# Feed-forward part of a hybrid decoder layer: order of two products, and which engine reads PSUM when

## The chip, the cores and the metric

One core of a Trainium2 chip runs the whole layer in one launch. The metric is device time in microseconds from the start of the launch to its end; the kernel before takes 745.95 us, the median of three runs (745.78 to 746.09).

## The reference, cut to what matters

The layer is a token mixer (attention and an mLSTM merged by gates) followed by a SwiGLU feed-forward part; the change is in the second. With 512 tokens, a model width of 1024 and a hidden width of 2816, all in float32:

```
h = h + merged @ w_out                       # token mixer, 512 x 1024
u = rms_norm(h, norm_ffn_g)
g, up = split(u @ w_gate_up)                 # 1024 -> 2 x 2816
h = h + (silu(g) * up) @ w_down              # 2816 -> 1024
out = rms_norm(h, norm_final_g)
```

## The kernel before

**Three products for one.** Every float32 operand is split into a high half (rounded to the format that TensorE multiplies at once) and a low half (the rest), so each product is three matmuls: high x high, low x high, high x low. ScalarE writes the high half of a weight tile (its copy in the helper `act_`, line 148 or 153), VectorE subtracts to get the low half (line 732 in the gated steps, 776 in the down steps).

**Seven products for eight.** The feed-forward matrices are multiplied as 2 x 2 blocks by a scheme of the Strassen-Winograd kind: seven block products named W11, S1, S2, W12, S3, S4, W22 after their weight operand, where S1 to S4 are sums of weight blocks made on VectorE (lines 740, 741 and 771). The sums of the results are formed partly by letting several products accumulate in one PSUM bank and reading partial sums out in between.

**Gated steps ("gu", 22 of them, one for each 128 hidden columns).** The blocks are halves of the 1024 inputs by halves of the tokens, and the two output blocks of a weight tile are gate and up. A product is 12 matmuls of 256 columns (`prod`, lines 784 to 786). X, one PSUM tile (pool `mm`, three buffers), first takes W11 and is copied to `s12` by ScalarE; then S2 is added into it and the sum copied again; then S3, copied to `x3` and added to Z on VectorE (line 835); then W22. Z (pool `s`, three buffers) takes S1 and later S4. Y (pool `acc`) takes W12. A product may only go on into a bank whose earlier sum has been read out. `gu_first` emits W11, `gu_main` S1 to S3, `gu_last` S4, W22 and the SiLU product, which goes through three or five more VectorE operations (even and odd steps) to the operands of the down product.

**Down steps ("ds", five).** Each takes four hidden tiles; a product is 2 token tiles x 6 matmuls of 512 columns (`ds_prod`, lines 897 to 899), with two X, two Z and the same chain of partial sums. Results are scaled by the tokens' inverse root mean square (`r`, `nr`) and added to the residual in DRAM by accumulating DMAs of GpSimd's queue. The last down step (`ds_end`) adds into the residual held in SBUF, takes in the last two hidden tiles by plain products (`last`), and ends with the final norm of four token blocks: VectorE's `add_`, ScalarE's `square`, Ln and Exp for the root, three VectorE operations (`newton`), then `apply` (one half on VectorE, one on ScalarE) and the DMA out.

**The order of work.** `plan` lays the products in a row and gives each a due time in ns: 1440 for a gated product, 2720 for a down product (two times 1360). `at(key, product, offset)` makes that time plus an offset the priority of the instructions that follow. A scheduler at build time fills each engine's queue by these priorities among what is ready by its own times; on the chip each queue runs in the order so fixed. Weights are prepared at offsets before their product (high half -1800, low half -800, sums -3800). Buffers are tiles from pools: ten tiles for split weights, seven for raw ones, 34 small ones.

The order of the products in a gated step, and the step between neighbours, is set in `plan`:

```
seq += [(x, w) for w in ("S1", "S2", "W12", "S3")]
after = [(ITEMS[j + 1], "W11")]
seq += (after if x[0] == "gu" else []) + [(x, w) for w in ("S4", "W22")] + (after if x[0] == "ds" else [])
```

Of the kernel before, what the change touches and what calls it, by code (L numbers as in the profile page):

```python
# [11 lines left out]
AF = mybir.ActivationFunctionType  # L12
# [59 lines left out]
NG = 5  # L72
DS_AFTER = {4: 0, 8: 1, 12: 2, 16: 3, 21: 4}

H_OFF, L_OFF, S_OFF, U_OFF, E_OFF, O_OFF, D_OFF, S4_OFF = 1800, 800, 3800, 0, 3000, 1500, 1500, 10000

PRE = 120

ITEMS = []
# [5 lines left out]
def hybrid_layer_kernel(ctx: ExitStack, tc, xT, wall, wgu, wds, wdl, g3v, vecs, wgates, consts, rope, out):  # L85
# [17 lines left out]
    def slot(dt=F32, name="a"):  # L103
        return act.tile([P, S], dt, name=nm(name), tag="A")
# [11 lines left out]
    def mmb():  # L116
        return psum.tile([P, S], F32, name=nm("mm"), tag="mm", bufs=3)

    def sb():
        return psum.tile([P, S], F32, name=nm("s"), tag="S", bufs=3)  # L120
# [25 lines left out]
    def act_(out_, in_, func, **kw):  # L146
        if func not in SETS:
            return A.activation(out_, in_, func, **kw)  # L148
        table(SETS[func])
        if ph["manual"]:  # L150
            return A.activation(out_, in_, func, **kw)
        with tc.issue_after(ph["load"]):
            i = A.activation(out_, in_, func, **kw)
        ph["ins"].append(raw_ins(i))
        return i
# [546 lines left out]
    def plan():  # L702

        t = 0
        LONG = {"W12": 4, "LAST": 1, "W22": 4, "S4": 5}
        seq = [(ITEMS[0], "W11")]
        for j, x in enumerate(ITEMS):
            if j == len(ITEMS) - 1:
                seq += [(x, w) for w in ("S1", "S2", "W12", "S3", "LAST", "W22", "S4")]
                continue  # L710
            seq += [(x, w) for w in ("S1", "S2", "W12", "S3")]
            after = [(ITEMS[j + 1], "W11")]
            seq += (after if x[0] == "gu" else []) + [(x, w) for w in ("S4", "W22")] + (after if x[0] == "ds" else [])
        for x, w in seq:
            clock["at"][x, w] = t
            t += 1440 if x[0] == "gu" else 1360 * LONG.get(w, 2) if x == ITEMS[-1] else 2720
        clock["end"] = t

    def at(key, w, off=0):
        t = clock["at"][key, w] + off  # L720
        tc.cur_priority = clock["base"] + (t if t > 0 else t // PRE)
# [56 lines left out]
    def prod(ps, w, o, first=False):  # L778

        wh, wl = w  # L780
        for k in range(4):
            c = slice(k * P, (k + 1) * P)
            bh, bl = bop(o, k)
            T.matmul(ps, wh[:, c], bh, start=first and k == 0, stop=False, skip_group_check=not first)  # L784
            T.matmul(ps, wl[:, c], bh, start=False, stop=False, skip_group_check=not first)  # L785
            T.matmul(ps, wh[:, c], bl, start=False, stop=k == 3, skip_group_check=not first)  # L786
# [3 lines left out]
    def gu_first(i):  # L790
        key = ("gu", i)
        g = sw[key]
        at(key, "W11")
        g["X"] = mmb()[:, 0:HS]
        prod(g["X"], g["W11"], 0, first=True)
        at(key, "S2")
        g["s"] = slot(name="s12")
        act_(g["s"][:, A_], g["X"], AF.Copy)

    def gu_main(i):  # L800

        key = ("gu", i)
        g = sw[key]
        x, s12 = g["X"], g["s"]
        at(key, "S1")
        z = g["Z"] = sb()[:, 0:HS]
        prod(z, g["S1"], 1, first=True)
        at(key, "S2")
        prod(x, g["S2"], 4)
        at(key, "S3")  # L810
        act_(s12[:, B_], x, AF.Copy)
        at(key, "W12")
        y = accb()[:, 0:HS]
        prod(y, g["W12"], 2, first=True)
        if i == 0:
            residual()
            rb2 = st["rb2"] = rstd_rows([ssum[2]])

            pr = sb()
            for t in range(4):  # L820
                T.transpose(pr[:, 4 * t : 4 * t + 4], rb2[0:4, t * P : (t + 1) * P], con[0:4, C_ID : C_ID + 4])
            st["rc"], st["nrc"] = (cst.tile([P, 4], F32, name=n_) for n_ in ("rc2", "nrc2"))
            V.tensor_copy(st["rc"], pr[:, 0:16:4])
            V.tensor_scalar(st["nrc"], pr[:, 0:16:4], -1.0, None, op0=ALU.mult)
        at(key, "W22", U_OFF)
        u = g["u"] = slot(name="up")
        V.tensor_tensor(u[:, A_], y, s12[:, A_], op=ALU.subtract)
        at(key, "S3")
        prod(x, g["S3"], 5)
        at(key, "S4")  # L830
        t = g["t"] = slot(name="gt")
        xs_ = slot(name="x3")[:, A_]
        act_(xs_, x, AF.Copy)
        at(key, "S4")
        V.tensor_tensor(t[:, B_], z, xs_, op=ALU.add)

# [69 lines left out]
    def ds_run(n):  # L908

        key = ("ds", n)  # L910
        w = sw.pop(key)["w"]
        r, nr = ([st[x][:, t : t + 1] for t in range(4)] for x in ("rc", "nrc"))
        Lo, Hi = slice(0, S), slice(S, D)
        to = lambda t, c, s: nc.gpsimd.dma_start(h1d[t][:, c], s, accum_op=ALU.add)
        two = range(2)
        X = [mmb() for t in two]
        s1, s2, x3 = [], [], []
        for t in two:
            at(key, "W11", 1360 * t)
            ds_prod(X[t], w["W11"], n, 0, t, first=True)  # L920
            at(key, "S2", 1360 * t)
            s1.append(slot(name="s1"))
            act_(s1[t], X[t], AF.Copy, scale=r[t])
        Z = [sb() for t in two]
        for t in two:
            at(key, "S1", 1360 * t)
            ds_prod(Z[t], w["S1"], n, 1, t, first=True)
        for t in two:
            at(key, "S2", 1360 * t)
            ds_prod(X[t], w["S2"], n, 4, t)  # L930
            at(key, "S3", 1360 * t)
            s2.append(slot(name="s2"))
            act_(s2[t], X[t], AF.Copy, scale=r[t + 2])
        for t in two:
            at(key, "W12", 1360 * t)
            y = accb()
            ds_prod(y, w["W12"], n, 2, t, first=True)
            at(key, "W12", 1360 * t + D_OFF)
            V.scalar_tensor_tensor(s1[t], y, r[t], s1[t], op0=ALU.mult, op1=ALU.subtract)
            to(t, Lo, s1[t])  # L940
        for t in two:
            at(key, "S3", 1360 * t)
            ds_prod(X[t], w["S3"], n, 5, t)
            at(key, "W22", 1360 * t)
            x3.append(slot(name="x3"))
            act_(x3[t], X[t], AF.Copy, scale=r[t + 2])
            at(key, "S4", 1360 * t)
            V.scalar_tensor_tensor(x3[t], Z[t], r[t + 2], x3[t], op0=ALU.mult, op1=ALU.add)
            to(t + 2, Hi, x3[t])
        for t in two:  # L950
            at(key, "S4", 1360 * t)
            ds_prod(Z[t], w["S4"], n, 3, t)
            at(key, "S4", 1360 * t + D_OFF)
            V.scalar_tensor_tensor(s2[t], Z[t], nr[t + 2], s2[t], op0=ALU.mult, op1=ALU.subtract)
            to(t + 2, Lo, s2[t])
        for t in two:
            at(key, "W22", 1360 * t)
            ds_prod(X[t], w["W22"], n, 6, t)
            at(key, "W22", 1360 * t + D_OFF)
            o = slot(name="c21")  # L960
            act_(o, X[t], AF.Copy, scale=r[t])
            to(t, Hi, o)
        hb[n] = None

    def ds_end():
# [12 lines left out]
        def add_(t, j, ps, c, d=slice(0, S)):  # L978

            h = hs[t][j][:, d]  # L980
            V.scalar_tensor_tensor(h, ps[:, d], c, h, op0=ALU.mult, op1=ALU.add)

        def square(t, j, d=slice(0, S)):
            s = v_()
# [24 lines left out]
        def last(ps, t, j, first=False, d=slice(0, S)):  # L1009

            q, c = slice(t * P, (t + 1) * P), slice(j * S + d.start, j * S + d.stop)
            for k in range(LK):
# [3 lines left out]
                T.matmul(ps[:, d], ah[:, q], wl[:, c], start=False, stop=False, **g)  # L1016
                T.matmul(ps[:, d], al[:, q], wh[:, c], start=False, stop=k == LK - 1, **g)

        X, Z = [mmb() for t in two], [sb() for t in two]
        for t in two:  # L1020
            at(key, "W11", U * t)
# [33 lines left out]
        for t in two:  # L1055
            at(key, "W22", 2 * U * t)
            ds_prod(X[t], w["W22"], n, 6, t)
            last(X[t], t, 1)
            at(key, "W22", 2 * U * t + 1000)
            times_g(t, 0)  # L1060
            at(key, "W22", 2 * U * (t + 1) + 200)
            add_(t, 1, X[t], r[t])
            square(t, 1)
            q, v, _ = rstd(t, "W22", 2 * U * (t + 1) + 2000)
            apply(t, newton(q, v, v_), 1)
        at(key, "S4")
        ds_prod(Z[0], w["S4"], n, 3, 0)
        last(Z[0], 2, 0)
# [2 lines left out]
        at(key, "S4", 2 * U + 200)  # L1071
        add_(2, 0, Z[0], nr[2])
        square(2, 0)
        q, v, _ = rstd(2, "S4", 2 * U + 2000)
        q2 = newton(q, v, v_)
        y = accb()
        lo, hi = slice(0, HS), slice(HS, S)
        at(key, "S4", 2 * U)
# [10 lines left out]
        at(key, "S4", 9 * U // 2)  # L1089
        last(y, 3, 1, first=True, d=hi)  # L1090
        at(key, "S4", 5 * U + 200)
        add_(3, 1, y, nr[3], hi)
        square(3, 1, hi)
        q, v, i = rstd(3, "S4", 5 * U + 800)
        with tc.issue_after(raw_ins(i[0])), tc.issue_after(raw_ins(i[1])):
            apply(2, q2, 0)
            times_g(3, 0)
        apply(3, newton(q, v, v_), 1)

# [527 lines left out]
```

## Time and profile before

| | |
|---|---|
| median of 3 runs | 745.95 us (745.78 to 746.09) |
| profiled execution | 745.64 us, of which the span from first to last instruction is 743.9 us |
| busy share of the span | TensorE matmul 99%, weight loads 86%, VectorE 84%, ScalarE 58%, GpSimd 8% |
| first feed-forward product, end of the last matmul | 400.3 us, 736.4 us |
| chain that ended last | TensorE 95%, VectorE 2%, ScalarE 1%, DMA 1% |

PE is TensorE's matmul row, PEld its row of weight loads, DVE is VectorE, ACT ScalarE, POOL GpSimd. A row of a product names its PSUM tile by pool: mm is X, s is Z, acc is Y. Matmuls are pipelined, so a matmul's duration is longer than the distance to the next one: distances are read from start to start.

### The profile page before, as it was taken

Reading aid. Unit: us, or ns where it says so; the run is one execution under the profiler, and the core shown is the slowest. Engines: PE = TensorE matmul, PEld = TensorE weight load, DVE = VectorE, ACT = ScalarE, POOL = GpSimd, SP = SyncE. Lnnn points to the kernel's source line nnn. Section 1 sums busy time; section 2 is a strip of 40 time slices with the busy share of each in tenths; the row PEclk is TensorE's granted clock in tenths of the full one; section 3 lists DMA queues with packets and bytes.
Section 4 is the critical chain, followed back from the end, with each engine's and each line's share of the span. In section 5 each row is a group of like instructions: output and inputs, shape, how many; then the busy total and the mean of one; then the engine's idle time right before and its main releaser. Section 6 shows DMA issues by size and latency. Waiting matters only on the chain.

```text
span 743.9 us, 11459 instructions
## 1 busy us (share of the span) xinstructions
PE 733.4 (99%) x4236; PEld 636.7 (86%) x4236; DVE 622.2 (84%) x1076; ACT 431.7 (58%) x745; POOL 59.3 (8%) x78
## 2 busy tenths in 40 slices
PE   9999999999999999999999999999999999999995
PEld 5788888888888888888888998899899899899984
DVE  6897786899986878476778899999989989988897
ACT  7534767578754447532446555755755666556454
POOL 0002010000000000000000000400310210130000
PEclk9999999999999999999999999999999999999998
DMA  8777554322332212524667344984895596497403
GB/s 328 278 225 209 180 183 112 115 106 79 135 116 104 84 59 85 198 86 137 166 187 206 112 129 124 215 266 90 206 276 142 136 283 181 115 239 216 165 1 113
DMA packets 50839, 118.70 MB, mean 160 GB/s; under 512 B 4944, under 2 KB 9688, under 8 KB 50784
## 3 DMA queue, kind: packets, MB, share of 16 engines
q1 hardware_dynamic: 36832, 88.82, 34.5%
q0 software_dynamic: 9440, 26.77, 18.4%
q10 hardware_dynamic: 4512, 2.39, 1.1%
q8 instruction: 33, 0.54, 0.3%
q14 instruction: 22, 0.18, 0.1%
HBM read 101.16 MB, written 16.81 MB: 159 GB/s over the span
## 4 chain that ended last, share of the span: by engine, by line
PE 95%; DVE 2%; ACT 1%; DMA 1%; issue 1%; SPq 0%; DVEq 0%; ACTq 0%
PE mm L201 12%; PE mm L202 12%; PE mm L203 12%; PE mm L784 6%; PE mm L786 6%; PE mm L785 6%; PE s L784 3%; PE s L786 3%; PE s L785 3%; PE mm L897 3%; PE mm L898 2%; PE mm L899 2%; PE mm L470 1%; PE mm L471 1%; PE acc L785 1%; PE acc L784 1%
## 5 line engine op out<-in xcount | busy, mean ns | idle before, releaser
L148 ACT ACTIVATE wh<-raw 128x1024 fp32r<-128x1024 f32 x58 | 61.3, 1058 | 67.5 <-PE mm L202 64.9
L161 DVE TENSOR_TENSOR wl<-raw,wh 128x1024 fp32r<-128x1024 f32 x58 | 70.5, 1220 | 9.9 <-ACT wh L148 9.2
L784 PE MATMUL mm<-bq,w 128*128 128x256 f32 x264 | 76.1, 288 | 0.4
L786 PE MATMUL mm<-bq,w 128*128 128x256 f32 x264 | 74.7, 283 | 0.0
L785 PE MATMUL mm<-bq,w 128*128 128x256 f32 x264 | 74.7, 283 | 0.0
L148 ACT ACTIVATE w<-s 128x1024 fp32r<-128x1024 f32 x44 | 46.6, 1060 | 35.0 <-DVE s L741 16.1
L732 DVE TENSOR_TENSOR w<-s,w 128x1024 fp32r<-128x1024 f32 x44 | 53.8, 1222 | 9.4 <-ACT w L148 7.7
L201 PE MATMUL mm<-u,wh 128*128 128x512 f32 x136 | 55.0, 405 | 0.3 <-DVE ga L563 0.3
L784 PEld LDWEIGHTS mm<-bq,w 128*128 128x128 f32 x264 | 50.5, 191 | 3.3 <-ACT x L148 1.9
L203 PE MATMUL mm<-u,wh 128*128 128x512 f32 x136 | 53.3, 392 | 0.0
L202 PE MATMUL mm<-u,wl 128*128 128x512 f32 x136 | 53.1, 391 | 0.0
L203 PE MATMUL mm<-ul,wh 128*128 128x512 f32 x136 | 53.0, 390 | 0.0
L202 PE MATMUL mm<-uh,wl 128*128 128x512 f32 x136 | 53.0, 390 | 0.0
L201 PE MATMUL mm<-uh,wh 128*128 128x512 f32 x136 | 52.9, 389 | 0.0
L693 POOL DMA_DIRECT2D s<-in_wgu_dram x22 | 19.4, 880 | 395.8 <-DVE ga L585 123.3
L785 PEld LDWEIGHTS mm<-bq,w 128*128 128x128 f32 x264 | 50.6, 192 | 0.1
L786 PEld LDWEIGHTS mm<-bq,w 128*128 128x128 f32 x264 | 50.6, 192 | 0.0
L784 PE MATMUL s<-bq,w 128*128 128x256 f32 x176 | 50.2, 285 | 0.0
L786 PE MATMUL s<-bq,w 128*128 128x256 f32 x176 | 49.9, 283 | 0.0
L785 PE MATMUL s<-bq,w 128*128 128x256 f32 x176 | 49.8, 283 | 0.0
L148 ACT ACTIVATE w<-raw 128x1024 fp32r<-128x1024 f32 (+2 forms) x45 | 43.5, 974 | 10.6 <-PE s L785 5.9
L148 ACT ACTIVATE w<-sw 128x1024 fp32r<-128x1024 f32 x20 | 21.2, 1061 | 31.2 <-DVE sw L771 30.9
(407 smaller groups left out, 2239.2 us busy)
## 6 DMA issues: line engine op xcount, KB each, us to landing
raw<-in_wall_dram SPq DMA_DIRECT2D x59, 512.0 KB, 3.6
s<-in_wgu_dram SPq DMA_DIRECT2D x22, 512.0 KB, 4.5
s<-in_wgu_dram POOLq DMA_DIRECT2D x22, 512.0 KB, 5.9
raw<-in_wgu_dram SPq DMA_DIRECT2D x22, 512.0 KB, 4.2
raw<-in_wds_dram SPq DMA_DIRECT2D x20, 512.0 KB, 9.6
w<-in_wgu_dram SPq DMA_DIRECT2D x22, 256.0 KB, 7.6
h1d<-s POOLq DMA_DIRECT2D x16, 256.0 KB, 10.0
R<-scr POOLq DMA_DIRECT2D x4, 896.0 KB, 4.7
```

The costliest lines, as they stand in the source:

```text
L148: return A.activation(out_, in_, func, **kw)
L161: V.tensor_tensor(l, src, f(h), op=ALU.subtract)
L201: T.matmul(ps, wh[:, c], rh[j], start=start and j == 0, stop=False)
L202: T.matmul(ps, wl[:, c], rh[j], start=False, stop=False)
L203: T.matmul(ps, wh[:, c], rl[j], start=False, stop=stop and j == n - 1)
L693: nc.gpsimd.dma_start(s13, wgu[i][:, 512:1536].rearrange("p (x c) -> p x c", x=2), accum_op=ALU.add)
L732: V.tensor_tensor(dst[1], src, f(dst[0]), op=ALU.subtract)
L784: T.matmul(ps, wh[:, c], bh, start=first and k == 0, stop=False, skip_group_check=not first)
L785: T.matmul(ps, wl[:, c], bh, start=False, stop=False, skip_group_check=not first)
L786: T.matmul(ps, wh[:, c], bl, start=False, stop=k == 3, skip_group_check=not first)
L897: T.matmul(ps, bh, wh[:, d], start=first and k == 0, stop=False, skip_group_check=not first)
L898: T.matmul(ps, bh, wl[:, d], start=False, stop=False, skip_group_check=not first)
```

## The change

In the gated steps S2 comes before S1, in the plan and in the code. Z is copied out by ScalarE as soon as S1 is done, into the B half of the tile `gt`; when S3 is done VectorE adds X, read from PSUM, to that copy. Before, Z stayed in PSUM, ScalarE copied X after S3, and VectorE added Z, read from PSUM. The same is done in the down steps, where the copy of Z is scaled by the tokens' factor. The reads of PSUM get as due time the modelled end of the product they read (its own time plus 1440, or 1360 for each token tile; the fused operation after S3 in the down steps plus 1500) in place of the start of a later product. After a down step, W11 of the next gated step now stands before S4 and W22, as it already did after a gated step.

At the end, block 1's scaling has its ScalarE part queued behind block 2's Exp and a later due time on both engines; block 2's root is planned 1000 ns earlier, and its scaling is queued on VectorE behind the last addition instead of behind block 3's first scalar operation, and on ScalarE no longer behind block 3's Exp.

```
@@ plan
-            seq += [(x, w) for w in ("S1", "S2", "W12", "S3")]
-            after = [(ITEMS[j + 1], "W11")]
-            seq += (after if x[0] == "gu" else []) + [(x, w) for w in ("S4", "W22")] + (after if x[0] == "ds" else [])
+            seq += [(x, w) for w in (("S2", "S1") if x[0] == "gu" else ("S1", "S2")) + ("W12", "S3")]
+            seq += [(ITEMS[j + 1], "W11"), (x, "S4"), (x, "W22")]
@@ gu_first
-        at(key, "S2")
+        at(key, "W11", R_OFF)
         g["s"] = slot(name="s12")
         act_(g["s"][:, A_], g["X"], AF.Copy)
@@ gu_main
+        at(key, "S2")
+        prod(x, g["S2"], 4)
+        at(key, "S2", R_OFF)
+        act_(s12[:, B_], x, AF.Copy)
         at(key, "S1")
         z = g["Z"] = sb()[:, 0:HS]
         prod(z, g["S1"], 1, first=True)
-        at(key, "S2")
-        prod(x, g["S2"], 4)
-        at(key, "S3")
-        act_(s12[:, B_], x, AF.Copy)
+        at(key, "S1", R_OFF)
+        gt = g["t"] = slot(name="gt")
+        act_(gt[:, B_], z, AF.Copy)
...
         at(key, "S3")
         prod(x, g["S3"], 5)
-        at(key, "S4")
-        t = g["t"] = slot(name="gt")
-        xs_ = slot(name="x3")[:, A_]
-        act_(xs_, x, AF.Copy)
-        at(key, "S4")
-        V.tensor_tensor(t[:, B_], z, xs_, op=ALU.add)
+        at(key, "S3", R_OFF)
+        V.tensor_tensor(gt[:, B_], x, gt[:, B_], op=ALU.add)
@@ ds_run
-            at(key, "S2", 1360 * t)
+            at(key, "W11", 1360 * t + RD_OFF)
             s1.append(slot(name="s1"))
             act_(s1[t], X[t], AF.Copy, scale=r[t])
...
             ds_prod(Z[t], w["S1"], n, 1, t, first=True)
+            at(key, "S1", 1360 * t + RD_OFF)
+            x3.append(slot(name="x3"))
+            act_(x3[t], Z[t], AF.Copy, scale=r[t + 2])
...
-            at(key, "S3", 1360 * t)
+            at(key, "S2", 1360 * t + RD_OFF)
             s2.append(slot(name="s2"))
             act_(s2[t], X[t], AF.Copy, scale=r[t + 2])
...
             ds_prod(X[t], w["S3"], n, 5, t)
-            at(key, "W22", 1360 * t)
-            x3.append(slot(name="x3"))
-            act_(x3[t], X[t], AF.Copy, scale=r[t + 2])
-            at(key, "S4", 1360 * t)
-            V.scalar_tensor_tensor(x3[t], Z[t], r[t + 2], x3[t], op0=ALU.mult, op1=ALU.add)
+            at(key, "S3", 1360 * t + D_OFF)
+            V.scalar_tensor_tensor(x3[t], X[t], r[t + 2], x3[t], op0=ALU.mult, op1=ALU.add)
@@ ds_end
             q, v, _ = rstd(t, "W22", 2 * U * (t + 1) + 2000)
-            apply(t, newton(q, v, v_), 1)
+            qs.append(newton(q, v, v_))
+            if t == 0:
+                apply(0, qs[0], 1)
...
-        q, v, _ = rstd(2, "S4", 2 * U + 2000)
-        q2 = newton(q, v, v_)
+        q, v, i = rstd(2, "S4", 2 * U + 1000)
+        qs.append(newton(q, v, v_))
+        at(key, "S4", 2 * U + 800)
+        with tc.issue_after(raw_ins(i[1])):
+            apply(1, qs[1], 1)
...
-        add_(3, 1, y, nr[3], hi)
+        i = add_(3, 1, y, nr[3], hi)
         square(3, 1, hi)
+        with tc.issue_after(raw_ins(i)):
+            apply(2, qs[2], 0)
         q, v, i = rstd(3, "S4", 5 * U + 800)
-        with tc.issue_after(raw_ins(i[0])), tc.issue_after(raw_ins(i[1])):
-            apply(2, q2, 0)
+        with tc.issue_after(raw_ins(i[0])):
             times_g(3, 0)
```

`issue_after` holds the block's instructions behind the named one in that one's engine queue, in order only. `R_OFF` is 1440, `RD_OFF` 1360, `D_OFF` 1500. `add_` now returns its instruction.

## Rows read from the trace of the kernel before

**Rows 1.** Busy time by stretch: us, then each engine's (instructions), PEclk, DMA share, GB/s.

```profile
418.00:452.00 34.00, 34.00 (x276) 33.49 (x275) 31.80 (x56) 20.64 (x33) 1.74 (x2) 1.00 0.45 133
...
473.00:513.00 40.00, 39.90 (x317) 38.93 (x316) 36.36 (x62) 24.75 (x39) 6.33 (x8) 1.00 0.86 226
```

**Rows 2.** Waits of PE and of PEld, 400 to 744: total us, times, longest.

```profile
PE mm L897 <- ACT s L148: 0.5, 1, 0.5
...
PEld mm L897 <- ACT s L148: 2.2, 6, 0.7
PEld mm L784 <- ACT x L148: 1.9, 7, 0.3
PEld mm L897 <- ACT x L148: 1.2, 4, 0.3
PEld mm L784 <- ACT s L148: 1.2, 5, 0.4
PEld acc L898 <- DVE w L776: 0.3, 1, 0.3
```

**Rows 3.** Timeline of the weight loader around W22 of a gated step: start, duration.

```profile
492.75 0.19 PEld L786 LDWEIGHTS s<-bq,w 128*128 128x128 f32 x1
493.25 0.19 PEld L784 LDWEIGHTS mm<-bq,w 128*128 128x128 f32 x1 [0.30 <-ACT x L148]
493.35 0.19 PEld L785 LDWEIGHTS mm<-bq,w 128*128 128x128 f32 x1
```

**Rows 4.** Timeline of the weight loader in a down step, 529.6 to 530.3.

```profile
529.64 0.19 PEld L899 LDWEIGHTS mm<-w,acl 128*128 128x128 f32 x1
530.13 0.19 PEld L897 LDWEIGHTS mm<-w,ac 128*128 128x128 f32 x1 [0.30 <-ACT x L148]
530.23 0.19 PEld L898 LDWEIGHTS mm<-w,ac 128*128 128x128 f32 x1
```

**Rows 5.** Timeline of TensorE: first matmuls of products that follow one another, and a recurrence.

```profile
531.62 0.39 PE L897 MATMUL s<-w,ach 128*128 128x512 f32 x1
...
534.34 0.39 PE L897 MATMUL mm<-w,ac 128*128 128x512 f32 x1
...
537.13 0.28 PE L784 MATMUL mm<-bq,w 128*128 128x256 f32 x1
...
538.57 0.28 PE L784 MATMUL acc<-bq,w 128*128 128x256 f32 x1
...
553.59 0.39 PE L784 MATMUL mm<-bq,w 128*128 128x256 f32 x1
```

**Rows 6.** VectorE's addition after S3: ns min/median/max, first and last start, shapes.

```profile
L835 DVE TENSOR_TENSOR gt<-s,x x22: 415/418/425, 410.8 to 706.7; 128x256 f32<-128x256 f32 x22
```

**Rows 7.** Timeline of ScalarE: copies out of PSUM and the weights ahead of them.

```profile
491.86 1.06 ACT L148 ACTIVATE w<-s 128x1024 fp32r<-128x1024 f32 x1 [0.66 <-DVE s L741]
492.83 0.37 ACT L148 ACTIVATE x<-mm 128x256 f32<-128x256 f32 x1
...
523.24 1.25 ACT L148 ACTIVATE s<-mm,rc 128x512 f32<-128x512 f32 x2
```

**Rows 8.** Timeline: VectorE's low half for S2, and S2's first matmul.

```profile
432.75 1.23 DVE L732 TENSOR_TENSOR w<-s,w 128x1024 fp32r<-128x1024 f32 x1 [0.19 <-ACT w L148]
...
436.02 0.28 PE L784 MATMUL mm<-bq,w 128*128 128x256 f32 x1
```

**Rows 9.** Waits of ScalarE before copies out of PSUM, 400 to 736.

```profile
ACT x L148 <- PE mm L786: 4.8, 7, 1.8
ACT s L148 <- PE mm L786: 4.6, 9, 0.9
```

**Rows 10.** Timeline of the end: ScalarE's Exp of block 3, and VectorE.

```profile
737.99 0.20 ACT L153 ACTIVATE v<-v 128x1 f32<-128x1 f32 x1
...
738.13 0.69 DVE L1007 TENSOR_TENSOR h<-h,g 128x512 f32<-128x512 f32 x1
738.73 0.15 DVE L319 TENSOR_TENSOR v<-v 128x1 f32<-128x1 f32 x1
```

More of the change, by code (lines that the diff above doesn't have):

```diff
@@ L73 @@
 DS_AFTER = {4: 0, 8: 1, 12: 2, 16: 3, 21: 4}
-H_OFF, L_OFF, S_OFF, U_OFF, E_OFF, O_OFF, D_OFF, S4_OFF = 1800, 800, 3800, 0, 3000, 1500, 1500, 10000
+H_OFF, L_OFF, S_OFF, U_OFF, E_OFF, O_OFF, D_OFF, S4_OFF, R_OFF, RD_OFF = 1800, 800, 3800, 0, 3000, 1500, 1500, 10000, 1440, 1360
 PRE = 120
@@ L980, in add_ @@
             h = hs[t][j][:, d]
-            V.scalar_tensor_tensor(h, ps[:, d], c, h, op0=ALU.mult, op1=ALU.add)
+            return V.scalar_tensor_tensor(h, ps[:, d], c, h, op0=ALU.mult, op1=ALU.add)
         def square(t, j, d=slice(0, S)):
@@ L1017, in last @@
                 T.matmul(ps[:, d], al[:, q], wh[:, c], start=False, stop=k == LK - 1, **g)
+        qs = []
         X, Z = [mmb() for t in two], [sb() for t in two]
```

## The prediction

> **What bounds the kernel now.** I read the page first, then the busy time by stretch, then the waits of the weight loader, VectorE and ScalarE, and last the timeline around single waits. In the feed-forward part TensorE is busy almost throughout; VectorE is at 31.80 of 34 us and 36.36 of 40 us, ScalarE at 24.75 of 40 us, and the granted clock is 1.00, its upper level of 2.4 GHz [rows 1]. So TensorE sets the time, with VectorE close behind it, and only two things can give time back: gaps between matmuls, and the 7.5 us behind the last one (736.4 to 743.9). The clock has nothing to give.
>
> The matmul row hides the gaps: it shows one wait in the whole part, 0.5 us. The weight loader shows 22 waits, 6.5 us, on ScalarE's copies out of PSUM (x is the copy after S3, s the copies after W11 and S2), against one of 0.3 us on VectorE [rows 2]. The Trainium skill warns of this ("Perfetto Trace Analysis", the opening note on roofline): matmul busy time is a bad measure because matmuls are pipelined, and loader busy time a good one. By the matmul row the feed-forward edits could return 0.5 us, by the loader row some ten times that; the trace sides with the loader, as the starts below show.
>
> **What the waits cost.** In the gated steps a product's 12 loads, and the matmuls with them, start 1.44 / 12 = 0.12 us apart [rows 5]. At 493.25 the product with W22 finds X not yet copied: loads start at 492.75, 493.25 and 493.35, 0.60 us where 0.24 would do, so a gap of 0.30 loses 0.36 [rows 3]. Twelve such waits (1.9 + 1.2 = 3.1 us of gap) cost 3.1 + 12 x 0.06 = 3.8 us. In the down steps they start 2.72 / 12 = 0.227 us apart [rows 5], and the gap at 530.13 (S3 behind the copy of X) gives 529.64, 530.13, 530.23: 0.59 for 0.45, a loss of 0.14 for the same 0.30 [rows 4]. Ten waits (2.2 + 1.2 = 3.4 us) cost 3.4 - 10 x 0.16 = 1.8 us. Together 5.6 us.
>
> From another side: the place at 493.25 recurs at 553.59, 60.34 us on, with four gated steps and one down step between. A gated product takes 1.44 us (537.13 to 538.57), so 28 take 40.32; a down product takes 2.72 (531.62 to 534.34), so 7 take 19.04 [rows 5]. That leaves 60.34 - 59.36 = 0.98 us lost a round, and in the 335 us from 400 to 735 us, 5.55 rounds, it makes 5.4 us. I take 5.5 us as all that the feed-forward edits can return.
>
> **The change part by part.** No product and no DMA is added or removed; the down steps' DMAs hang on the same VectorE results as before. Of ScalarE's three copies of 128x256 in a gated step three stay (one takes Z in place of X); VectorE's addition of 0.418 us stays one operation with one operand from PSUM [rows 6]. The trace has no such copy of Z; by the copy of X, of the same shape, it is 0.37 us [rows 7]. In the down steps it is the same with two wider copies and two fused operations. Engine work: 0. One SBUF tile a gated step goes; no wait names it: 0.
>
> What changes is how long each result may take before TensorE needs it.
> 1. *W22 into X* waited for ScalarE's copy of X, behind whatever stood in that queue: at 491.86 a copy of weights of 1.06 us, itself 0.66 late on VectorE, kept it until 492.83 [rows 7]. Now VectorE reads X when S3 is done, with W11 and S4 between S3 and W22, 2 x 1.44 = 2.88 us. The worst I see is one 1.23 us operation in progress and then 0.418, 1.65 us. Covered. S4 in turn needs only the copy of Z, made three products earlier.
> 2. *S3 into X* waited for the copy after S2 with one product between; now two, 2.88 us for a copy of 0.37.
> 3. *S2 into X (down steps)* waited for copies of W11's result that were placed at S2's own due time and ran at 523.24, the moment TensorE needed them [rows 7]. Now they are placed at W11's end, with both products of S1 to cover them.
> 4. *W11 of the next gated step* stands before S4 and W22 of a down step, so its weights are due 2 x 2.72 = 5.4 us earlier. Cost 0 while VectorE has its idle 3.6 in 40 us; if that is gone, rival one.
> 5. *S2 before S1*: its weights (two additions, one ScalarE copy, one subtraction on VectorE) are due 1.44 us earlier, S1's as much later. At the tightest place I find, the subtraction runs 432.75 to 433.98 and S2 starts at 436.02 [rows 8]: 2.04 us to spare, 0.60 after. Covered, with no more than that (rival two).
>
> Behind the moved copies on ScalarE wait the high halves of weights, and behind those VectorE's subtractions. ScalarE stood idle for TensorE before copies of X: 4.6 us in 9 and 4.8 us in 7 cases [rows 9], 0.5 to 0.7 us each, in an engine with 15 us idle in 40: I price it at 0 and keep the bad case as rival three.
>
> All 22 waits get a cover longer than the delays shown. Lower bound of the gain: nothing, if the waits only change place. Upper: 5.5 us. For what comes in their place I allow up to two waits of today's 0.36 us a round, 5.55 x 0.72 = 4.0 us, and take half, 2.0, because the one margin I could read is positive but small. Net -3.5 us.
>
> **The end.** Exp for the last block starts at 737.99 and takes 0.20; VectorE is then in a 0.69 us product with g from 738.13 and begins the last reciprocal root at 738.73, 0.54 us late [rows 10]. The change puts the scaling of block 2 and that product ahead: at best -0.5. Against it, ScalarE's share of block 2, or VectorE's scaling of block 1, may now stand in front of the chain; an operation of that kind is of the size of the 0.69, so at worst +0.7. I take -0.2, since the lateness is there and the new obstacle is not certain.
>
> **Sum.** -3.5 - 0.2 = -3.7. The profiled execution took 745.64 us (span 743.9 and 1.7 around it), 0.31 less than the median of 745.95. So 741.94 by the profiled execution, and 742.2 us by the median.
>
> **Rivals.** *One, VectorE takes it back.* It has 2.2 us idle in 34 and 3.6 in 40 [rows 1]. If its low halves come as late as TensorE now comes early, gaps on copies of X turn into gaps on weights. Against: only 0.3 us of such gaps today [rows 2]. Between half the net gain and all of it lost: 744.0 to 747.4, most likely 745.5. Chance 0.14.
>
> *Two, S2's weights are late (slower).* The place is the subtraction before S2. If one more operation of 1.23 us is ordered ahead of it, S2 starts 1.23 - 0.60 = 0.63 us late in each of the 11 odd steps, where VectorE has more to do: +6.9, so 742.2 + 6.9 = 749.1. It decides from 3.7 / 22 = 0.17 us a step on. For it: 0.60 of margin, and VectorE 91 to 94% busy. Against: the subtraction is planned 1.44 us earlier too. Chance 0.16, 747.5 to 751.
>
> *Three, the copies block ScalarE.* A copy placed at a product's modelled end stands first in its queue until TensorE is done. At 0.5 to 0.7 us a time [rows 9] the high half behind it comes late by S2's whole margin of 0.60, and half of the 22 steps get a 0.36 us gap back: 4.0 us, so 746.2, no measurable change. Chance 0.06. The Trainium skill ("PSUM — Partial Sum Buffer", Engine vs sequencer instructions) has ScalarE's queue strictly first in, first out, which this rival needs; the trace agrees, since the copy of X at 492.83 waited out the late copy of weights ahead of it.
>
> **Chances and range.** The forecast's case (most waits gone, none new of size) 0.64: 739.9 (745.95 less 5.5 and 0.5) to 744.0. Cases one and three 0.20, two 0.16. What cannot be told from no change is about 0.2%, 1.5 us: faster is below 744.5, slower above 747.4. The low edge of case one still counts as faster: faster 0.66, same 0.18, slower 0.16. The range leaves out case two and the very edges of the others: 740.0 to 747.2.
>
> **What the profile will show.** Right: loader waits on ScalarE in the feed-forward part from 6.5 to under 2 us; the round of four gated steps and one down step from 60.34 to between 59.4 and 59.8; VectorE's and ScalarE's busy times within 1%; the last reciprocal root begun within 0.2 us of Exp's end. Wrong: new loader waits on VectorE's weights of over 2 us in all, above all before S2; rounds still of 60.3; or a ScalarE that waits much longer for TensorE before its copies while VectorE waits longer for high halves.

## The result, and the profile after

The changed kernel took 742.46 us (median of 6 runs, 741.91 to 742.66) and the kernel before 746.15 us on the same chip (6 runs, 745.78 to 746.84). The ratio is 0.9948, interval 0.9935 to 0.9961: 3.7 us faster. The prediction said 742.2. The profiled execution took 742.66 us with a span of 740.5, 3.4 less than the span before.

First the waits of the weight loader and of TensorE, 400 to 744 us, in the changed kernel (total us, times, longest). These answer to [rows 2].

```profile
PEld acc L784 <- DVE w L731: 0.9, 1, 0.9
PEld mm L783 <- ACT s L148: 0.7, 2, 0.4
PEld s L783 <- ACT gt L148: 0.2, 1, 0.2
...
PE acc L784 <- DVE w L731: 0.7, 1, 0.7
```

Of 22 waits on ScalarE, 6.5 us, three are left, 0.9 us. One long wait is new: 0.9 us on VectorE, once. Gaps shorter than 0.15 us are not in these lists; two that matter are read further down.

What that does to the beat shows in the same matmul of W11 (L784 mm<-bq,w11l) wherever it comes back after four gated steps and one down step:

```profile
477.12 0.28 PE L784 MATMUL mm<-bq,w11l 128*128 128x256 f32 x1
...
536.35 0.28 PE L783 MATMUL mm<-bq,w11h 128*128 128x256 f32 x1
536.48 0.39 PE L783 MATMUL mm<-bq,w 128*128 128x256 f32 x1
536.70 0.28 PE L784 MATMUL mm<-bq,w11l 128*128 128x256 f32 x1
...
596.28 0.28 PE L784 MATMUL mm<-bq,w11l 128*128 128x256 f32 x1
```

Two rounds, each of 59.58 us, against 60.34 in the kernel before. From the first product of the feed-forward part to TensorE's last matmul it is 332.5 us against 336.1. The part in front of it, whose code is unchanged, was 0.6 us longer in this execution (first product at 400.90 against 400.31; in all the traces of this document between 399.9 and 401.5), and the tail behind the last matmul 0.37 shorter (7.10 against 7.47): -3.6 - 0.37 + 0.6 = -3.4, the difference of the spans.

The same stretches as in [rows 1], with the same columns:

```profile
418.00:452.00 34.00, 33.31 (x273) 32.83 (x273) 31.09 (x56) 20.39 (x34) 1.73 (x2) 1.00 0.46 134
473.00:513.00 40.00, 40.00 (x319) 39.26 (x318) 36.90 (x61) 24.66 (x40) 5.40 (x7) 1.00 0.85 221
```

In the second stretch the loader went from 38.93 to 39.26 us and TensorE stands at all 40; the granted clock is 1.00 as before. In the first one the loader has lost a little: the new 0.9 us wait lies in it. Its timeline, loader first, then VectorE:

```profile
434.16 0.19 PEld L784 LDWEIGHTS acc<-bq,w 128*128 128x128 f32 x1 [0.89 <-DVE w L731]
...
432.88 1.22 DVE L731 TENSOR_TENSOR w<-raw,w 128x1024 fp32r<-128x1024 f32 x1
```

A matmul of W12 (acc) stands here ahead of the S4 product of the step before, as a filler, and needs W12's low half, which VectorE finishes at 434.10.

ScalarE's waits before its copies of gated products out of PSUM, 400 to 736 us, to be set against [rows 9]:

```profile
ACT s L148 <- PE mm L785: 30.7, 18, 2.7
```

ScalarE now stands 30.7 us before such copies, where it stood 9.4. A copy is first in its queue and waits for TensorE, instead of TensorE waiting for it.

The end (ScalarE's Exp of the last block, then VectorE), answering to [rows 10]:

```profile
735.12 0.20 ACT L153 ACTIVATE v<-v 128x1 f32<-128x1 f32 x1
...
735.35 0.16 DVE L319 TENSOR_TENSOR v<-v 128x1 f32<-128x1 f32 x1
```

Exp ends at 735.32 and the reciprocal root begins at 735.35: 0.03 us late, where it was 0.54.

### The profile page after: what moved, and what is told of

It reads as the page before. It is cut to its first block, busy times and chain, and to the rows that moved or that the text cites. A ratio compares the mean times of both kernels' runs of the same rounds, so it can differ in the third digit from the quotient of the medians.

```text
span 740.5 us, 11458 instructions
## 1 busy us (share of the span) xinstructions
PE 730.5 (99%) x4236; PEld 638.0 (86%) x4236; DVE 620.5 (84%) x1076; ACT 428.5 (58%) x745; POOL 59.2 (8%) x78
## 4 chain that ended last, share of the span: by engine, by line
PE 93%; DVE 3%; DMA 2%; ACT 1%; issue 1%; SPq 0%; DVEq 0%; ACTq 0%
PE mm L201 12%; PE mm L202 12%; PE mm L203 12%; PE mm L783 6%; PE mm L784 5%; PE mm L785 5%; PE s L783 3%; PE s L784 3%; PE s L785 3%; PE mm L895 2%; PE mm L896 2%; PE mm L897 2%; PE mm L470 1%; PE mm L471 1%; PE mm L472 1%; PE acc L784 1%
## 5 line engine op out<-in xcount | busy, mean ns | idle before, releaser
L784 PE MATMUL mm<-bq,w 128*128 128x256 f32 x264 | 74.9, 284 | 0.0
L731 DVE TENSOR_TENSOR w<-s,w 128x1024 fp32r<-128x1024 f32 x44 | 53.7, 1220 | 11.0 <-ACT w L148 9.5
L784 PEld LDWEIGHTS mm<-bq,w 128*128 128x128 f32 x264 | 50.6, 192 | 0.1
L784 PE MATMUL s<-bq,w 128*128 128x256 f32 x176 | 49.8, 283 | 0.0
L148 ACT ACTIVATE s<-mm 128x256 f32<-128x256 f32 x44 | 16.6, 376 | 30.7 <-PE mm L785 30.7
```

The costliest lines, as they stand in the source:

```text
L731: V.tensor_tensor(dst[1], src, f(dst[0]), op=ALU.subtract)
```

## The experiments

All were timed in five rounds beside the kernel before, whose median in these batches was 746.1 to 746.3. "The swap" is: ScalarE copies Z early and VectorE reads X from PSUM, where ScalarE copied X late and VectorE read Z.

**The due times alone** (kernel before, the planned times of the copies and of the additions to them as in the change; one of eight such lines).

```diff
-            at(key, "S2", 1360 * t)
+            at(key, "W11", 1360 * t + RD_OFF)
             s1.append(slot(name="s1"))
```

> The kernel before with the due times alone moved: every read of PSUM gets the modelled end of the product it reads; the products' order, the copy of X after S3 and the end stay. Theory A (the gain is cover: how much other work lies between a partial sum and the product that needs its bank): S3 still has one product of cover after S2 and S4 one after the addition to Z, so loader waits on ScalarE or VectorE stay above 3 us and the time at 744.0 to 745.5. Theory B (the copies were simply placed too late, and the order and the copy of Z do nothing): waits under 1.5 us, 742.8, which is the changed kernel plus some 0.35 for the old end.

746.01 us, ratio 0.9999 (0.9990 to 1.0008). Every engine runs the same instructions in the same order as in the kernel before, and all the loader's waits have the totals of [rows 2]. The planned times of reads, as moved here, decide nothing.

**S1 before S2 again** (changed kernel, the first product order as before).

```diff
-            seq += [(x, w) for w in (("S2", "S1") if x[0] == "gu" else ("S1", "S2")) + ("W12", "S3")]
+            seq += [(x, w) for w in ("S1", "S2") + ("W12", "S3")]
```

> The changed kernel with S1 before S2 again in the gated steps, all else as changed. Theory A: one product less between S2 and S3, the copy behind S2 becomes late again at one place a round (0.23 us a round, 5.5 rounds): 743.3 to 744, waits <-ACT s back before mm<-bq,w. Theory B: 742.5, no such waits. Theory C (S2's weights are the tight place; S2 first costs): faster than the changed kernel, 741.5, because the wait of 0.9 us on W12's low half and the filler products go.

742.64 us, ratio 0.9953 (0.9941 to 0.9966), not to be told from the change, with the same three kinds of loader waits. The precedence of S2 carries nothing here.

**X copied again** (changed kernel with the swap undone in both kinds of steps).

```diff
-            V.scalar_tensor_tensor(x3[t], X[t], r[t + 2], x3[t], op0=ALU.mult, op1=ALU.add)
+            x3.append(slot(name="x3"))
+            act_(x3[t], X[t], AF.Copy, scale=r[t + 2])
+            V.scalar_tensor_tensor(x3[t], Z[t], r[t + 2], x3[t], op0=ALU.mult, op1=ALU.add)
```

> The changed kernel with X copied by ScalarE after S3 and added to Z by VectorE again, in gated and down steps, but due at S3's end. Theory A: S4 then needs copy and addition done within one product (1.44 us for 0.37 + 0.42 and two queues), so waits of about 0.3 us come back at S4 once or twice a round: 744 to 745. Theory B: 742.5.

752.55 us, ratio 1.0087 (1.0073 to 1.0101): slower than before. The loader's waits, 400 to 770 us:

```profile
PEld s L783 <- ACT w L148: 4.3, 1, 4.3
PEld mm L895 <- ACT s L148: 2.1, 7, 0.4
PEld mm L783 <- ACT x L148: 1.7, 7, 0.3
PEld mm L895 <- ACT x L148: 1.1, 4, 0.3
PEld mm L783 <- ACT s L148: 0.8, 3, 0.4
```

The last four lines, 5.7 us, are nearly those of [rows 2]: without the swap the waits are back. What makes this kernel slower than the one before stands at a single place. The loader waits 4.3 us, from 463 to 467 us, for the high half of a gated step's weights, and the granted clock then shows its lower level, 0.50 (1.2 GHz), here after the stretch and its busy times as in [rows 1]:

```profile
469.00:472.00 3.00, 3.00 (x9) 2.33 (x8) 1.30 (x2) 0.69 (x1) 1.77 (x2) 0.50 1.00 244
```

Matmuls of 512 columns start 0.43 us apart there, where 0.23 is usual. Read from the starts of the matmuls, that place loses 6.6 us, and all the others together 6.0, against 6.6 in the whole of the kernel before. Whether undoing the swap has to bring such a place is not shown.

**The old end** (changed kernel with the end as before).

```diff
-        with tc.issue_after(raw_ins(i)):
-            apply(2, qs[2], 0)
...
+        with tc.issue_after(raw_ins(i[0])), tc.issue_after(raw_ins(i[1])):
+            apply(2, q2, 0)
```

> The changed kernel with the end (last down step and final norm) of the kernel before. If the end gave 0.35 us as the two traces say (from the last addition to the last DMA 4.32 us before, 3.97 after), the time is 742.8, the last matmul stands where it does in the changed kernel, and the root is late by 0.5 us again. If the end gave nothing by itself: 742.5.

743.00 us, ratio 0.9958 (0.9944 to 0.9971), 0.5 above the change. The intervals overlap, but the traces agree: the tail behind the last matmul is 7.51 us here, 7.46 to 7.55 in three other runs with the old end (the swap alone and its two halves, below) and 7.10 in the changed kernel. The end is worth 0.4 to 0.5 us.

**The swap alone** (kernel before, with the swap in both kinds of steps; old order, old end).

```diff
+        act_(gt[:, B_], z, AF.Copy)
...
-        xs_ = slot(name="x3")[:, A_]
-        act_(xs_, x, AF.Copy)
-        V.tensor_tensor(t[:, B_], z, xs_, op=ALU.add)
+        V.tensor_tensor(gt[:, B_], x, gt[:, B_], op=ALU.add)
```

> The kernel before with one edit: Z copied to SBUF behind S1 and X read by VectorE after S3, in gated and down steps; order of products, the other due times and the end as before. Theory D (this swap alone makes the feed-forward gain): the time of the changed kernel with the old end, 743.0, within 0.5. If S2 first or W11 before S4 carries a part: 744 to 745.

743.29 us, ratio 0.9956 (0.9943 to 0.9970). With the end's 0.5 taken off, 742.8, that is nearly the change. Its loader waits, 400 to 770 us:

```profile
PEld mm L784 <- ACT s L148: 1.3, 5, 0.4
PEld acc L785 <- DVE w L732: 0.9, 1, 0.9
PEld s L784 <- ACT gt L148: 0.2, 1, 0.2
PEld mm L896 <- ACT s L148: 0.2, 1, 0.2
```

**Half the swap**: in the gated steps alone, then in the down steps alone, each in the kernel before.

> The swap of Z and X in the gated steps alone, all else before. By the waits of the trace before, the gated places lose 0.36 + 0.23 us a round and some 0.8 at the start, 3.4 in all, and one new wait of 0.9 on W12's low half comes: 743.6 to 744.4, with the down steps' waits of 3.4 us still there. If the two swaps only work together: 745.5 or more.

> The swap in the down steps alone, all else before. By the waits of the trace before it returns up to 1.8 us (the ten waits before down products): 744.3 to 745.0, the gated waits of 3.1 us still there. If the down steps' waits come from ScalarE running behind because of the gated steps: 746.1, nothing.

Gated alone 745.86 us, ratio 0.9993 (0.9984 to 1.0002); down alone 746.98 us, 1.0008 (0.9999 to 1.0017). Neither half returns anything that can be measured, while both together return 2.9 us. The loader's waits of the gated half, then of the down half:

```profile
PEld mm L784 <- ACT s L148: 2.1, 8, 0.4
PEld mm L896 <- ACT s L148: 1.8, 6, 0.5
...
PEld acc L785 <- DVE w L732: 0.9, 1, 0.9
```

```profile
PEld mm L897 <- ACT s L148: 2.4, 4, 0.7
PEld mm L784 <- ACT x L148: 1.7, 6, 0.3
PEld mm L784 <- ACT s L148: 0.7, 2, 0.4
```

In the gated half the seven waits on x in gated steps (1.9 us) are gone, but those on s there grew from 1.2 to 2.1 us and the 0.9 us of the filler came. In the down half the four waits on x are gone and the six on s have become four longer ones. One of these in the down half (its loader, then its ScalarE):

```profile
524.42 0.19 PEld L897 LDWEIGHTS mm<-w,ach 128*128 128x128 f32 x1 [0.58 <-ACT s L148]
```

```profile
520.38 0.63 ACT L153 ACTIVATE gt<-gt 128x512 f32<-128x512 f32 x1 [4.03 <-DVE gt L856]
...
523.70 1.25 ACT L148 ACTIVATE s<-mm,rc 128x512 f32<-128x512 f32 x2
```

The product W11 of the down step was done near 514, yet its copies (s) run at 523.70: ScalarE stood 4.0 us at the SiLU of the gated step ahead, with the copies behind it, and S2 found X not free. The 0.58 us is too long to hide: the matmul row has this wait too, 1.6 us in four. In the gated half one of the longest waits, 0.40 us at 551.75, is of a like kind: S2 was done near 550, but its copy ran at 551.33, behind a copy of weights that had itself waited 0.78 us for VectorE's sum.

**Those copies ahead of the SiLU**, once with the down half of the swap and once with the whole change. For this the down step's W11 and its copies are written into a function of their own that runs before `gu_last`; the cut shows the SiLU alone.

```diff
+        with ExitStack() as es:
+            if "s1" in st:
+                es.enter_context(tc.issue_after(st.pop("s1")))
+            act_(t, t, AF.Silu)
```

> The swap in the down steps alone, and the two ScalarE copies of a down step's first product now queued ahead of the SiLU of the gated step before it. With the swap in the down steps alone the round was 60.73 us and TensorE's loader waited once in each down step for such a copy (0.57 us; the matmul behind it 0.37 us), because ScalarE stood 4.0 us at that SiLU with the copies behind it. Theory (the copies are late only through ScalarE's strict order): the wait goes in four steps, about 0.6 us each, round near 60.1, time near 744.5. Rival (something else is late there, or the wait moves to the SiLU's own readers): 746.4 to 747.6 as without it.

> The whole change, with the same two copies queued ahead of that SiLU. Theory: the changed kernel has no wait left on these copies (loader waits on ScalarE 0.9 us in the whole part, round 59.58 with 0.16 us above the pure matmul time), so nothing is to be won: 742.1 to 742.9. Rival one (an early copy moves work forward): under 741.8. Rival two (a later SiLU makes the hidden units late): over 743.3.

769.28 us, ratio 1.0312 (1.0298 to 1.0326), and 743.81 us, 0.9967 (0.9955 to 0.9980). In both the theory fell, in the first by 25 us. In the first kernel the largest waits are now these:

```profile
PEld s L900 <- ACT x L148: 7.8, 8, 1.7
PEld acc L785 <- DVE w L732: 5.9, 8, 0.9
PEld mm L784 <- ACT x L148: 5.9, 7, 1.3
PEld mm L784 <- ACT w11h L148: 3.4, 4, 1.1
```

The down steps' waits on copies of W11 and S2 are gone, and other work of ScalarE came late: the copies of Z (first line), X's copies of gated steps, high halves of weights. The edit also changed the planner's order of products (S2 of the down step now ahead of its W12), so the loss can't be laid to the later SiLU alone. This one copy pulled forward did not mend the queue. With the whole change the same edit cost 1.35 us, mostly in four waits of S3 for the copies after S2 (s), 1.6 us. The time is in rival two's range, but these are not waits for hidden units, and the order of products changed here in the same way: why it cost is open.

**W11 of the next gated step later** (changed kernel, planned behind S4 and W22 of a down step as before).

```diff
-            seq += [(ITEMS[j + 1], "W11"), (x, "S4"), (x, "W22")]
+            after = [(ITEMS[j + 1], "W11")]
+            seq += (after if x[0] == "gu" else []) + [(x, w) for w in ("S4", "W22")] + (after if x[0] == "ds" else [])
```

> The changed kernel with W11 of the next gated step planned behind S4 and W22 of a down step again. My prediction priced this edit at 0, because the kernel before already ran that product early: 742.5, same waits. If the planned place matters: W22 of the down step comes one product sooner after S3, waits on VectorE's read of X of 0.3 to 0.7 us a round, 744 to 746.

742.45 us, ratio 0.9948 (0.9935 to 0.9960): the same as the change.

**W12 behind S4** (changed kernel; a gated step's W12 is queued on TensorE behind S4 of the step before, which removes the filler at 434 us).

```diff
+        with ExitStack() as es:
+            if "s4" in st:
+                es.enter_context(tc.issue_after(st["s4"]))
+            prod(y, g["W12"], 2, first=True)
```

> The whole change, with each gated step's W12 product queued on TensorE behind S4 of the step before, which takes away the few matmuls of W12 that ran ahead of S4 at 434 us and waited 0.9 us there for VectorE's low half. Theory: that wait goes and nothing takes its place, 741.5 (0.95 less than 742.46). Rival (those few matmuls fill a wait in other steps, which now opens): 742.3 to 743.5.

741.37 us (741.21 to 741.65), ratio 0.9936 (0.9923 to 0.9948), 1.1 below the change and the fastest of all; the single times don't overlap with the change's (741.91 to 742.66). Its loader waits, 400 to 770 us, and the place of the new one:

```profile
PEld mm L783 <- ACT s L148: 0.7, 2, 0.4
PEld mm L783 <- DVE gt L837: 0.5, 1, 0.5
```

```profile
434.23 0.41 DVE L837 TENSOR_TENSOR gt<-mm,gt 128x256 f32<-128x256 f32 x1
...
434.70 0.19 PEld L783 LDWEIGHTS mm<-bq,w 128*128 128x128 f32 x1 [0.50 <-DVE gt L837]
```

The 0.9 us wait is gone; in its place W22 waits 0.5 us for VectorE to read X. From the first product to the last matmul it takes 331.8 us, 4.3 less than the kernel before and 0.7 less than the change.

**Every product in the written order** (changed kernel; each gated product queued behind the one before it, no fillers).

```diff
+            if st.get("prev"):
+                es.enter_context(tc.issue_after(st["prev"]))
...
+        st["prev"] = raw_ins(i)
```

> The whole change, with every gated product queued on TensorE behind the gated product before it in the written order, so that no product is begun early as a filler. Theory (after the swap the operands are in time in the written order): the 0.9 us wait goes and the rest stays, 741.3 to 742.2. Rival (the swap only pays because the queues' order lets other products fill the places where ScalarE is late): over 743.5, with loader waits on ScalarE back.

757.37 us, ratio 1.0147 (1.0127 to 1.0167); the trace is of an execution of 754.56. The rival was right. Its largest line of loader waits, then the loader and ScalarE at one of its four places behind a down step:

```profile
PEld mm L786 <- ACT s L148: 12.0, 5, 3.3
```

```profile
541.57 0.19 PEld L786 LDWEIGHTS mm<-bq,w 128*128 128x128 f32 x1 [2.18 <-ACT s L148]
541.98 0.19 PEld L787 LDWEIGHTS mm<-bq,w 128*128 128x128 f32 x1 [0.22 <-DVE w L731]
```

```profile
538.49 0.69 ACT L148 ACTIVATE c<-mm,rc 128x512 f32<-128x512 f32 x1 [4.05 <-PE mm L901]
...
541.14 0.37 ACT L148 ACTIVATE s<-mm 128x256 f32<-128x256 f32 x1
```

Behind a down step S2 comes first in the written order, and X's copy, which frees X for it, stands behind the copies of the down step's W22, before the first of which ScalarE stands 4.05 us. In the changed kernel ScalarE stands there as long, but TensorE runs S1 first, as a filler. The order that the planner makes of the written one is part of the gain.

## Why the prediction was right, and which of its steps were not

**The bound and the mechanism held.** TensorE sets the time, and the gaps are the loader's waits on ScalarE's copies. The swap takes them away: it alone gives 2.9 of the 3.7 us, and undoing it brings 5.7 of the 6.5 us of waits back. The page of the profile has VectorE at 620.5 us (622.2 before) and ScalarE at 428.5 (431.7), within 1% as said. All four signs of "right" came: 6.5 to 0.9 us of waits, a round of 59.58, the busy times, the root 0.03 us late.

**The gross gain of 5.5 us held.** The starts of the matmuls show every loss, also those behind gaps too short for the lists. By the prediction's own spacings, 0.120 us for 256 columns and 0.227 for 512, the 2331 matmuls from the first product to the last lose 6.6 us in the kernel before and 3.0 in the changed one. Of both sums 0.8 us lies in the first gated step, where the two kernels lose alike. The other 5.8 us is what the prediction put at 5.5. Its conversion of gaps was less good than its sum: by the starts the 22 waits cost 4.6 us, not 5.6, because four of the twelve in gated steps stand behind matmuls of 512 columns, where a gap costs less (last section), and lost only 0.05 to 0.22 us each; gaps too short for the list and small delays make up the rest.

**The allowance of 2.0 us for what comes in place of the waits held in size, by luck.** It was half of a range from 0 to 4.0 us, meant for up to two new waits of 0.36 us a round. What is left in the changed kernel is 2.2 us of another kind: 1.0 at the filler's wait of 0.9 us, 0.3 at the wait on `gt`, 0.3 in the last gated steps, and 0.6 behind the four down steps, 0.16 at each. So the feed-forward part gave 5.8 - 2.2 = 3.6, where 5.5 - 2.0 = 3.5 was predicted. The profile before could not show the filler; the planner made it anew.

The place behind a down step, in the changed kernel:

```profile
533.40 0.69 ACT L148 ACTIVATE c<-mm,rc 128x512 f32<-128x512 f32 x1 [4.05 <-PE mm L897]
...
535.61 1.23 DVE L731 TENSOR_TENSOR w<-s,w 128x1024 fp32r<-128x1024 f32 x1 [1.19 <-ACT w L148]
...
536.05 0.37 ACT L148 ACTIVATE s<-mm 128x256 f32<-128x256 f32 x1
...
536.23 0.19 PEld L783 LDWEIGHTS mm<-bq,w11h 128*128 128x128 f32 x1
...
536.48 0.19 PEld L783 LDWEIGHTS mm<-bq,w 128*128 128x128 f32 x1
...
536.71 0.19 PEld L785 LDWEIGHTS mm<-bq,w11h 128*128 128x128 f32 x1
...
536.89 0.19 PEld L784 LDWEIGHTS mm<-bq,w 128*128 128x128 f32 x1
```

ScalarE's copy of X after W11 ends at 536.42, and S2's first load (`mm<-bq,w`) starts at 536.48 instead of 536.35. VectorE's low half for S2 ends at 536.84, and the load that needs it starts at 536.89 instead of 536.83. This is most of the 0.22 us by which the round of 59.58 stays above the prediction's 59.36. The fastest kernel has the same two gaps, and a round of 59.57.

**Item 1 (W22 into X)** held in the changed kernel: the loader's list has no wait on VectorE's read. In the fastest kernel one of 0.5 us appears, so the cover is not as wide everywhere as 2.88 against 1.65 us said.

**Item 2 (S3 into X)** held, but not because S1 and S2 were exchanged, as the run with S1 first shows.

**Item 3 (S2 into X in down steps) failed as a mechanism.** The copies of W11 were to run at W11's end. They did not; ScalarE in the changed kernel:

```profile
521.54 1.25 ACT L148 ACTIVATE s<-mm,rc 128x512 f32<-128x512 f32 x2
...
525.24 0.69 ACT L148 ACTIVATE s<-mm,rc 128x512 f32<-128x512 f32 x1 [1.29 <-PE mm L897]
```

They run at 521.54, as late in the queue as in [rows 7]. Due times alone changed no queue. The waits went all the same: with X's copies out of the queue, the copy after S2 (525.24) stands first and waits 1.29 us for TensorE. That is the copy which counted: of the six waits on s in down steps of the kernel before, only the first, 0.66 us at 463.73, was S2's for a copy of W11; the other five were S3's for the copy after S2. A slip in the text of that section belongs here: at 530.13 [rows 4] it is W22, not S3, that waits for the copy of X; the loss of 0.14 us is the same.

**Item 4 (W11 early)**, priced at nothing, measured at nothing. **Item 5 (S2 before S1)** brought no gain, and no wait for S2's weights that is in the list. But the margin, 0.60 us at the place where the prediction read it, is used up behind each down step, where the low half is 0.05 us late. With all products in the written order S2's low half is 0.22 us late four times; rival two had 0.63.

**The end** was mis-sized: -0.2 predicted, -0.4 to -0.5 measured. The obstacle that was to take half of it back did not come in the changed kernel: the root is 0.03 us late. With X copied again it did: the same new end has a tail of 7.45 us there, as the last Ln stands 0.4 us behind a scaling on ScalarE.

**The rivals.** One, VectorE taking it back, appeared as a single 0.9 us wait. Two came in small: S2's low half is 0.05 us late at four places, not 0.63 at eleven. Three came as a mechanism and cost next to nothing: ScalarE's waits before copies went from 9.4 to 30.7 us, and VectorE's for high halves (`w`, from ScalarE, L732 before and L731 after) from 7.7 to 11.8 us, which the prediction listed among the signs of "wrong". None of these waits is in the loader's list; the late copy of X behind a down step, 0.11 us at four places, is the most that can be laid to them. "PSUM — Partial Sum Buffer" of the Trainium skill (Engine vs sequencer instructions) has ScalarE's queue strictly first in, first out; the runs agree, and where it does hurt is the 2.18 us above.

**What the prediction did not see** is that the gain isn't a sum over waits. It priced the waits of gated steps at 3.8 us and those of down steps at 1.8. Alone, the gated half gave 0.4 us and the down half -0.8, neither told from zero. For the down half the trace names the link, a SiLU with copies queued behind it; that it is the cause is argued, since the attempt to remove it changed the order of products too. In the gated half one place shows the copy behind late weights; why those came late, and with them why the waits on s in gated steps grew (1.2 to 2.1 us), stays open.

## What to carry to other kernels

Before trading an early copy against a late one, count what stands in the copying engine's queue, and take the late copy out of it in every stage that shares the queue: half of the edit here was worth nothing, the whole 2.9 us. Don't stop at the list of waits: gaps too short for it show in the distances between starts, and set against the sum of the products they tell what is left to gain. Planned times that changed no engine's order of instructions changed nothing here, so compare the orders before giving such an edit a price; and look for fillers that run ahead of their operands, since holding one back was worth another 1.1 us by the medians and 0.7 by the traces.

## What the runs showed of the hardware that was not expected

What a gap of the loader costs can't be read from its length alone: it went by the columns of the matmul in front of the gap. Behind 256 columns it cost more than its length, for two starts came late: 0.30 us cost 0.36 [rows 3], and 0.06 cost 0.11 (the starts at 536.35, 536.48 and 536.70 in the first section: 0.35 us where 0.24 is usual). So a gap too short for the list of waits cost about twice its length here.

Behind 512 columns it cost less: 0.30 us cost 0.14 inside a down step [rows 4], and 0.28 us cost 0.13 before a 256-column product (454.76 in the kernel before). In the down half of the swap the gap of 0.58 us stands in front of a 512-column product as well, but behind a 256-column matmul:

```profile
523.77 0.28 PE L786 MATMUL mm<-bq,w11h 128*128 128x256 f32 x1
524.42 0.50 PE L897 MATMUL mm<-w,ach 128*128 128x512 f32 x1 [0.37 <-ACT s L148]
524.75 0.39 PE L898 MATMUL mm<-w,ach 128*128 128x512 f32 x1
```

The two starts come 0.98 us after the first, where 0.12 + 0.23 = 0.35 is usual: 0.58 us cost 0.63. Four such waits cost more than the ten short ones that they replaced (round 60.73 against 60.34 us).

The granted clock fell to its lower level within a pause of TensorE of 4.1 us (X copied again), and the matmuls behind it paid for that as well: of the 6.6 us lost at that place 2 are theirs.
